# The down projection of a layer by seven block products instead of eight

## The chip, the cores and the metric

The kernel runs on one core of a Trainium2 chip. A core has five engines with an instruction queue each: TensorE (PE: matmuls from SBUF into eight banks of PSUM), VectorE (DVE), ScalarE (ACT), GpSimd (POOL) and SyncE (SP, here only transfers). The metric is device microseconds of one execution; a change is judged by several executions of both kernels on the same chip.

## What is computed

One layer on 512 tokens of width 1024, all in 32-bit floats: a token mixer of three branches, then a gated MLP with a causal convolution, each with a modulation worked out from a condition `c` and followed by a residual and a LayerNorm. The change is in the second half:

```python
D_MODEL = 1024; SEQ = 512; DEPTH = 1; D_FF = 2816; CONV_W = 3

def _conv_ffn(h, w_up, conv_w, conv_b, w_down):
    z = h @ w_up                                  # 512 x 5632
    S = z.shape[1]
    zp = jnp.pad(z, ((0, 0), (CONV_W - 1, 0), (0, 0)))
    zc = conv_b + conv_w[0] * zp[:, 0:S]
    for k in range(1, CONV_W):
        zc = zc + conv_w[k] * zp[:, k:k + S]
    val, gate = jnp.split(zc, 2, axis=-1)
    return (jax.nn.silu(gate) * val) @ w_down     # 512 x 2816 by 2816 x 1024

def reference(...):
    mod = silu(c) @ w_ada[l] + b_ada[l]
    sh_t, sc_t, gt_t, sh_f, sc_f, gt_f = jnp.split(mod, 6, axis=-1)
    ...
    h = _modulate(x, sh_f, sc_f)
    y = _conv_ffn(h, w_up[l], conv_w[l], conv_b[l], w_down[l])
    x = _layer_norm(ALPHA * x + gt_f[:, None, :] * y) * ln_f_g[l] + ln_f_b[l]
```

## The kernel before

**Products.** TensorE multiplies 32-bit numbers by a split: each operand is a rounded high part (`fp32r`, copied by ScalarE) and the rest (a difference on VectorE), and a product is three matmuls, high by low, low by high and high by high (`mm3`, L107; `mm_chunk`, L112). So every weight block costs a copy of ScalarE and a difference of VectorE before TensorE can use it. Weights come by SP's queue into a pool of three raw buffers of 128 x 1024 and are split into two buffers each of high and low parts (`wsplit`, L90; `scaled_chunk`, L1130). A planner (`make_plan`, L375) splits the chunk after the next one ahead.

**Stages in order of time.** Latent projections and attention (to about 200 us); the attention branch with the pooling inputs (`pool`, `merge(0, m)`); the pooling mixer; the spatial gating's `v` in two halves of four steps (`uv_half`, L979), where other work is hung behind the split of each step (`v_first`, `v_second`, L1004); the pooling branch (`merge(1, m)`); the spatial gating (`gated`); its branch (`merge(2, m)`); the output projection; the second modulation; the up projection of 44 chunks (22 pairs `i` of value and gate, from some 590 to 826 us); the down projection to 943 us; the normalized rows are stored while it closes.

**The up projection's end.** For each `i` ScalarE and VectorE form the convolution from PSUM, ScalarE the silu, GpSimd the product `val`; `val` (128 hidden rows x 512 tokens) is split into `f{i}h` and `f{i}l`, which stay in SBUF as the left operands.

**The down projection** is `project_out` (L1150, called at L1495) with 22 steps over the hidden dimension. Eight PSUM banks hold 4 token blocks of 128 x 2 halves of 512 columns. In 18 steps a weight row block of 128 x 1024 is loaded, multiplied by the gate `gt_f` on GpSimd (L1135, so that the gate costs nothing later), split, and used by 24 matmuls. The last four row blocks are split ahead and kept; then the banks are closed one after the other with 12 matmuls each, and `finish` (L1453) adds the residual of each bank, takes its statistics, and after both halves normalizes the row block and stores it. The last half is closed in two pieces of 256 columns.

**The gates.** `gate_rows` (L896) reduces the modulation (`ada_cols`), sends it to DRAM in one transposing transfer and reads it back as two rows spread over 128 partitions, for the mixer's gate (idx 0) and for the MLP's (idx 3).

**Pools** that the change uses: 48 tiles of 128 x 512 (`act_t`), 16 (`h_t`, the up projection's inputs until it ends), 8 (`pt_t`), 5 of 128 x 528 (`pad_t`), 8 PSUM banks (`ps`). An instruction that wants a tile waits until one is free. The order within each queue is made by the tile framework when the kernel is built; `tc.issue_after` puts an instruction behind another one of its engine, and `behind_split` puts work behind the newest weight split.

## Time and profile before

| | |
|---|---|
| median of 3 runs | 953.44 us (952.78 to 953.79) |
| the profiled execution: its own time | 953.06 us |
| its span, first to last instruction | 951.3 us |
| mean granted TensorE clock | 0.998 |
| bytes moved | 119.85 MB, 126 GB/s in the mean |
| weights of the down projection `d<-in_wdn` | 22 loads of 512 KB, 3.4 us to landing |

The profile lists each instruction with engine, line, the tile written and the tiles read, its duration, and the wait before it. "Releaser" is the instruction whose end ended a wait. Busy times of a stretch are sums over the engine's instructions in it, and a number in brackets behind them counts the instructions. PE lines are matmuls, PEld lines the loading of their left operands; a few per cent of the matmul records can be missing.

### The profile page before, as it was taken

What the parts mean: (1) busy time and instruction counts of PE and PEld (TensorE: products, weight loads), DVE (VectorE), ACT (ScalarE), POOL (GpSimd) and SP (SyncE); (2) the same over time, 40 slices, a digit from 0 to 9 for tenths busy, and PEclk for the clock granted to TensorE, in tenths of its full rate; (3) what the DMA queues carried; (4) which work ended last, traced back from release to release, by engine and by line L of the source; (5) the groups of instructions that cost most, each with busy time, mean ns of one, the idle gap of its engine ahead of it and who ended that gap; (6) DMA issues with size and microseconds to landing.
All of it is one profiled execution on the core that took longest, in us unless ns stands there. A gap on an engine that the chain in (4) does not pass through costs nothing.

```text
span 951.3 us, 12080 instructions
## 1 busy us (share of the span) xinstructions
PE 937.2 (99%) x4516; PEld 791.0 (83%) x4516; DVE 597.0 (63%) x868; ACT 377.8 (40%) x619; POOL 292.0 (31%) x270
## 2 busy tenths in 40 slices
PE   7999999999999999999999999999999999999996
PEld 6988888888888888888888889988888888888885
DVE  7966668546676575677354589575655665633277
ACT  4576555533324322133322434654444444321121
POOL 4741121122341032302043713021111132756653
PEclk9999999999999999999999999999999999999999
DMA  9823112145436532664343440233344364432322
GB/s 320 326 65 108 57 36 83 45 133 153 134 100 228 183 99 100 190 205 138 111 134 132 156 155 23 68 121 123 111 133 133 113 84 138 132 111 89 107 71 88
DMA packets 46586, 119.85 MB, mean 126 GB/s; under 512 B 6144, under 2 KB 9664, under 8 KB 46528
## 3 DMA queue, kind: packets, MB, share of 16 engines
...
q0 software_dynamic: 1024, 1.19, 0.5%
...
## 4 chain that ended last, share of the span: by engine, by line
PE 94%; DMA 2%; DVE 1%; POOL 1%; issue 1%; ACT 1%; SPq 0%; POOLq 0%; DVEq 0%; ACTq 0%
PE pzu L115 7%; PE pzu L118 7%; PE pzu L116 7%; PE py L115 4%; PE py L118 4%; PE py L116 4%; PE pg L115 4%; PE pg L116 4%; PE pg L118 4%; PE pyd L1168 3%; PE pyd L1166 3%; PE pyd L1169 3%; PE lat L528 2%; PE pu L115 2%; PE pa L115 2%; PE pa L116 2%
## 5 line engine op out<-in xcount | busy, mean ns | idle before, releaser
L95 DVE TENSOR_TENSOR wupl<-wup,wuph 128x1024 fp32r<-128x1024 f32 x38 | 47.0, 1237 | 70.9 <-PE pzu L118 40.5
L1135 POOL TENSOR_TENSOR d<-d,gtf 128x512 f32<-128x512 f32 x44 | 74.5, 1716 | 35.8 <-DMA d<-in_wdn 35.1
L1441 POOL TENSOR_TENSOR zc<-zc 128x512 f32<-128x512 f32 x22 | 29.7, 1350 | 173.6 <-ACT zc L1440 172.4
L1140 DVE TENSOR_TENSOR dl<-d,dh 128x1024 fp32r<-128x1024 f32 x18 | 29.8, 1653 | 55.8 <-PE pyd L1166 51.6
L94 ACT CAST wuph<-wup 128x1024 fp32r<-128x1024 f32 x38 | 39.8, 1048 | 46.3 <-PE pzu L116 46.3
L94 ACT CAST wbh<-wb 128x1024 fp32r<-128x1024 f32 x24 | 25.2, 1051 | 69.2 <-PE py L116 50.4
L856 DVE SCALAR_TENSOR_TENSOR ada<-adar,cact,ada 128x512 f32<-128x512 f32 x56 | 50.1, 924 | 0.0
L419 POOL TENSOR_TENSOR mg<-mg,th 128x512 f32<-128x512 f32 x16 | 29.3, 1832 | 58.6 <-DVE th L416 58.5
L95 DVE TENSOR_TENSOR wgl<-wg,wgh 128x1024 fp32r<-128x1024 f32 x22 | 28.5, 1295 | 28.5 <-ACT wgh L94 16.5
L1139 ACT CAST dh<-d 128x1024 fp32r<-128x1024 f32 x18 | 18.9, 1051 | 62.0 <-PE pyd L1169 37.8
L1421 ACT ACTIVATE zc<-pzu,cols 128x512 f32<-128x512 f32 x44 | 34.1, 778 | 22.1 <-PE pzu L118 17.7
L95 DVE TENSOR_TENSOR wbl<-wb,wbh 128x1024 fp32r<-128x1024 f32 x24 | 31.1, 1294 | 14.9 <-ACT wbh L94 6.5
L775 POOL TENSOR_SCALAR pe<-pe,mx 128x128 f32<-128x128 f32 (+3 forms) x32 | 17.0, 534 | 69.3 <-DVE mx L774 43.2
L1424 DVE SCALAR_TENSOR_TENSOR zc<-pzu,cols,zc 128x511 f32<-128x511 f32 x44 | 32.6, 744 | 4.2 <-ACT zc L1421 4.2
L94 ACT CAST wgh<-wg 128x1024 fp32r<-128x1024 f32 x22 | 23.3, 1058 | 27.9 <-PE pg L116 20.3
L1428 DVE SCALAR_TENSOR_TENSOR zc<-pzu,cols,zc 128x510 f32<-128x510 f32 x44 | 32.6, 746 | 0.8
L1440 ACT ACTIVATE zc<-zc 128x512 f32<-128x512 f32 x22 | 13.9, 631 | 43.0 <-DVE zc L1428 43.0
L926 POOL TENSOR_TENSOR asum<-apad 128x527 f32<-128x527 f32 x8 | 12.3, 1540 | 54.7 <-ACT apad L921 28.1
L298 DVE SCALAR_TENSOR_TENSOR acc<-ada,cact,acc 128x256 f32<-128x256 f32 (+1 forms) x29 | 28.3, 975 | 1.2 <-DMA ada<-in_ada1p 0.2
L416 DVE SCALAR_TENSOR_TENSOR th<-th,py 128x512 f32<-128x512 f32 x16 | 11.0, 686 | 26.3 <-PE py L118 26.3
L1113 POOL TENSOR_TENSOR oraw<-oraw,gtt 128x512 f32<-128x512 f32 x6 | 11.1, 1872 | 41.4 <-DMA oraw<-in_wo 41.4
L1135 POOL TENSOR_TENSOR o<-o,gtt 128x512 f32<-128x512 f32 x10 | 18.1, 1831 | 12.1 <-DMA o<-in_wo 10.0
...
## 6 DMA issues: line engine op xcount, KB each, us to landing
...
```

The lines of the kernel that those rows point to most:

```text
L94: nc.scalar.copy(out=hi[:, :n], in_=raw[:, :n])
L95: ins = nc.vector.tensor_tensor(out=lo[:, :n], in0=raw[:, :n], in1=f(hi[:, :n]), op=ALU.subtract)
L115: nc.tensor.matmul(o, wh[:, c], xl[k], start=k == 0, stop=False)
L116: nc.tensor.matmul(o, wh[:, c], xh[k], start=False, stop=False)
L118: nc.tensor.matmul(o, wl[:, c], xh[k], start=False, stop=k == KT - 1)
L856: nc.vector.scalar_tensor_tensor(out=acc[n], in0=src, scalar=cact[:, k : k + 1], in1=acc[n], op0=ALU.mult, op1=ALU.add,)
L1135: nc.gpsimd.tensor_tensor(out=halves[n], in0=halves[n], in1=gt[n], op=ALU.mult)
L1140: nc.vector.tensor_tensor(out=lo, in0=raw, in1=f(hi), op=ALU.subtract)
L1421: nc.scalar.activation(t, pz, AF.Identity, bias=cols[:, cc + 3 : cc + 4], scale=cols[:, cc + 2 : cc + 3])
L1424: nc.vector.scalar_tensor_tensor(out=t[:, 1:512], in0=pz[:, 0:511], scalar=cols[:, cc + 1 : cc + 2], in1=t[:, 1:512], op0=ALU.mult, op1=AL ...
L1428: nc.vector.scalar_tensor_tensor(out=t[:, 2:512], in0=pz[:, 0:510], scalar=cols[:, cc : cc + 1], in1=t[:, 2:512], op0=ALU.mult, op1=ALU.add,)
L1441: nc.gpsimd.tensor_tensor(out=val, in0=val, in1=gate, op=ALU.mult)
```

## The change

The product A·B of the down projection is cut into 2 x 2 blocks: 512 tokens into two halves, the hidden dimension into even and odd row blocks (11 pairs `p`), 1024 columns into two halves. It is then computed by seven block products instead of eight, each the sum over the pairs. The weight combinations that this needs (`t3`, `wide`, `t4`) are made from the raw weights during the earlier stages and written to DRAM; the left combinations are made when `val` is ready. The products run in two sweeps over the pairs: first products 1, 5, 6 and 7 in eight PSUM banks, then 2, 3 and 4 in six. The left operands of the second sweep go to DRAM for nine of eleven pairs and are read back. Weights of the second sweep's last five pairs are split ahead, during the first sweep. The gate now multiplies bank sums; two of the eight half rows are complete after the first sweep, the other six are completed as the second sweep's banks close. The gate rows' way through DRAM uses a transpose on VectorE and four transfers.

```diff
@@ -893,11 +894,21 @@
...
-    def gate_rows(idx, c0, name):
-        ada_cols(idx, c0, False, name)
+    def gate_line(idx, c0, name):
+        square = const.tile([P, 32], F32, name=name + "s")
+        turned = const.tile([P, 32], F32, name=name + "t")
+        nc.gpsimd.memset(square, 0.0)
+        ada_cols(idx, c0, False, name, square[:, :KT])
+        nc.vector.transpose(out=turned, in_=square)
         line = dr.tile([KT, P], F32, name=name + "r")
-        nc.gpsimd.dma_start(out=line.rearrange("j c -> c j"), in_=modulation[idx])
-        flat = line.rearrange("(o j) c -> o (j c)", o=1)
+        for i in range(4):
+            nc.gpsimd.dma_start(
+                out=line[:, 32 * i : 32 * i + 32], in_=turned[32 * i : 32 * i + KT, :]
+            )
+        gate_row[idx] = line
+
+    def gate_rows(idx, name):
+        flat = gate_row.pop(idx).rearrange("(o j) c -> o (j c)", o=1)
...
@@ -948,6 +959,32 @@
...
+    HP = NP // 2
+    wide_t = [dr.tile([P, D], F32, name=f"wt21{p}") for p in range(HP)]
+    t3_t = [dr.tile([P, 512], F32, name=f"wt3{p}") for p in range(HP)]
+    t4_t = [dr.tile([P, 512], F32, name=f"wt4{p}") for p in range(HP)]
+
+    def combine_weights(p):
+        b = []
+        for k in (2 * p, 2 * p + 1):
+            for n in range(2):
+                blk = act_t(f"wb{k}{n}", F32)
+                nc.sync.dma_start(
+                    out=blk, in_=A["wdn"][k * P : (k + 1) * P, n * 512 : (n + 1) * 512]
+                )
+                b.append(blk)
+        b11, b12, b21, b22 = b
+        for dst, x, y, op in (
+            (b22, b22, b12, ALU.subtract), (b12, b12, b11, ALU.subtract),
+            (b11, b22, b11, ALU.add), (b21, b11, b21, ALU.subtract),
+        ):
+            ins = nc.vector.tensor_tensor(out=dst, in0=x, in1=y, op=op)
+        for dst, src in (
+            (t3_t[p], b22), (wide_t[p][:, 512:], b12), (wide_t[p][:, :512], b11), (t4_t[p], b21),
+        ):
+            nc.gpsimd.dma_start(out=dst, in_=src)
+        return ins
+
...
     pool(0)
     pool(1)
@@ -957,6 +994,8 @@
             pool(m + 1)
         merge(0, m, oT_hi, oT_lo, th0[m])
         behind_split(ada_piece, 0, m)
+        if m == 6:
+            behind_split(combine_weights, 0)
...
@@ -1004,6 +1043,8 @@
     def v_second(q):
...
+        if q:
+            combine_weights(q)
...
@@ -1040,8 +1081,10 @@
...
+        if m == 4:
+            behind_split(gate_line, 0, C_GT, "gtt")
+        if m % 2:
+            behind_split(combine_weights, 4 + m // 2)
...
@@ -1089,6 +1132,8 @@
...
     for g in range(KT):
+        if g == 2:
+            gate_rows(0, "gtt")
...
@@ -1108,6 +1153,8 @@
...
+        if m < 3:
+            behind_split(combine_weights, 8 + m)
...
@@ -1402,8 +1449,61 @@
...
+    left1 = []
+    left2 = {}
+    SPILLED = HP - 2
+    spill = [[dr.tile([P, 512], F32, name=f"ys{p}{i}") for i in range(3)] for p in range(SPILLED)]
+
+    def split256(dst, src):
+        nc.scalar.copy(out=dst[:, :256], in_=src)
+        nc.vector.tensor_tensor(out=dst[:, 256:], in0=src, in1=f(dst[:, :256]), op=ALU.subtract)
+
+    def first_left(p, v1):
+        xa = act_t(f"xa{p}")
+        split256(xa, v1[:, :256])
+        left1.append([xa])
+
+    def other_lefts(p, v1, v2):
+        d = pad_t("sd")
+        e = pad_t("se")
+        for dst, x, y, op in (
+            (e[:, :256], v1[:, 256:], v2[:, 256:], ALU.add),
+            (d[:, :256], e[:, :256], v1[:, :256], ALU.subtract),
+            (d[:, 256:512], v1[:, :256], v1[:, 256:], ALU.subtract),
+            (e[:, 256:512], v2[:, :256], d[:, :256], ALU.subtract),
+        ):
...
+        split256(xs, e[:, :256])
+        nc.scalar.copy(out=xh, in_=d[:, :512])
+        nc.vector.tensor_tensor(out=xl, in0=d[:, :512], in1=f(xh), op=ALU.subtract)
+        nc.scalar.copy(out=yh, in_=v2)
+        nc.vector.tensor_tensor(out=yl, in0=v2, in1=f(yh), op=ALU.subtract)
+        split256(ys, e[:, 256:512])
+        left1[p] += [xs, xh, xl]
+        if p >= SPILLED:
+            left2[p] = [yh, yl, ys]
+            return
+        for dst, src in zip(spill[p], (yh, yl, ys)):
+            nc.gpsimd.dma_start(out=dst, in_=f(src))
...
@@ -1431,43 +1531,209 @@
...
-        if i % 2 == 1 and i < 2 * KT:
-            ada_piece(3, i // 2)
-        if i == 2 * KT:
+        if 3 <= i < 3 + KT:
+            ada_wide_piece(3, i - 3)
+        if i == 3 + KT:
             ada_parts(3, "gtf")
-        if i == 2 * KT + 2:
-            gate_rows(3, C_GT + 8, "gtf")
+        if i == 5 + KT:
+            gate_line(3, C_GT + 8, "gtf")
+        if i == 5 + KT + 1:
+            gate_rows(3, "gtf")
         nc.scalar.activation(gate, gate, AF.Silu)
         nc.gpsimd.tensor_tensor(out=val, in0=val, in1=gate, op=ALU.mult)
-        ah = act_t(f"f{i}h")
-        al = act_t(f"f{i}l")
...
-        a_hi.append(ah)
-        a_lo.append(al)
...
-
-    lnfg = row_tiles(4, act_t, "lnfg")
-    lnfb = row_tiles(5, act_t, "lnfb")
...
+        if i % 2 == 0:
+            first_left(i // 2, val)
+            held[0] = val
+        else:
+            other_lefts(i // 2, held[0], val)
+
+
+    gt_f = [gate_row[3, n] for n in range(2)]
+    R2 = 5
+    lo_half, hi_half = slice(0, 512), slice(512, 1024)
+
+    def split_wide(parts, n, name):
+        hi = wp.tile([P, D], F32R, name=name + "h", tag="whi")
+        lo = wp.tile([P, D], F32R, name=name + "l", tag="wlo")
+        for raw, c in parts:
+            nc.scalar.copy(out=hi[:, c], in_=raw)
+            nc.vector.tensor_tensor(out=lo[:, c], in0=raw, in1=f(hi[:, c]), op=ALU.subtract)
+        return hi, lo
+
...
+    def sweep_step(p, chunks):
+        for (wh, wl), users in chunks:
+            for rest in range(2):
+                for t in range(2):
+                    for acc, (xh, xl), c in users:
+                        ts_ = slice(t * P, (t + 1) * P)
+                        if rest:
+                            nc.tensor.matmul(acc[t], xh[:, ts_], wl[:, c], start=False, stop=False)
+                        else:
+                            nc.tensor.matmul(acc[t], xh[:, ts_], wh[:, c], start=p == 0, stop=False)
+                            nc.tensor.matmul(acc[t], xl[:, ts_], wh[:, c], start=False, stop=False)
+
+    m1, m5, m6, m7 = ([ps(f"pd{c}") for _ in range(2)] for c in (1, 5, 6, 7))
+
+    def lefts1(p):
+        xa, xs, xh, xl = left1[p]
+        return {
+            1: (xa[:, :256], xa[:, 256:]), 5: (xs[:, :256], xs[:, 256:]),
+            6: (xh[:, :256], xl[:, :256]), 7: (xh[:, 256:], xl[:, 256:]),
+        }
+
+    def lefts2(p):
+        yh, yl, ys = left2[p]
+        return {
+            2: (yh[:, :256], yl[:, :256]), 4: (yh[:, 256:], yl[:, 256:]),
+            3: (ys[:, :256], ys[:, 256:]),
+        }
+
+    def reload(p):
+        left2[p] = [act_t(f"z{i}{p}") for i in range(3)]
+        for dst, src in zip(left2[p], spill[p]):
+            nc.gpsimd.dma_start(out=dst, in_=src)
+
+    ws2 = {}
+
+    def second_weights(p, alloc):
+        srcs = ((2, wdn_row(2 * p + 1, lo_half)), (3, wdn_row(2 * p + 1, hi_half)), (4, t4_t[p]))
+        raws = [(c, block(src, f"dr{c}", pt_t)) for c, src in srcs]
+        ws2[p] = {c: split_block(raw, f"d{c}{p}", alloc) for c, raw in raws}
+
+    ahead = [(second_weights, HP - R2, h_t)]
+    for i in range(R2 - 1):
+        ahead += [(second_weights, HP - R2 + 1 + i, act_t), (reload, i)]
+    ahead.append((reload, R2 - 1))
+    free = 1 + 6
+    for p in range(HP - 1):
+        rb = [block(wdn_row(2 * p, lo_half), "db0"), block(t3_t[p], "db1")]
+        ra = whole(wide_t[p], "da")
+        wb_ = split_wide(zip(rb, (lo_half, hi_half)), D, "db")
+        wa_ = split_wide(((ra, slice(0, D)),), D, "da")
+        x = lefts1(p)
+        sweep_step(p, (
+            (wb_, ((m1, x[1], lo_half), (m7, x[7], hi_half))),
+            (wa_, ((m6, x[6], lo_half), (m5, x[5], hi_half))),
+        ))
+        while ahead and free >= (need := 6 if ahead[0][0] is second_weights else 3):
+            work, *args = ahead.pop(0)
+            work(*args)
+            free -= need
+        free += 4
+    p = HP - 1
+    rb = [block(wdn_row(2 * p, lo_half), "db0"), block(t3_t[p], "db1")]
...
+    for work, *args in ahead:
+        work(*args)
...
+    def ordered(work):
+        with ExitStack() as order:
+            if last_product:
+                order.enter_context(tc.issue_after(last_product[0]))
+            last_product[:] = [work().ins]
+
+    u1, u3, u4, c22 = ([None] * 2 for _ in range(4))
+
+    def evacuate(c, t, acc):
+        if c == 1:
+            u1[t] = h_t(f"u1{t}", F32)
+            nc.scalar.copy(out=u1[t], in_=acc)
+        elif c == 6:
+            u4[t] = h_t(f"u4{t}", F32)
+            nc.vector.tensor_tensor(out=u4[t], in0=acc, in1=u1[t], op=ALU.add)
+        elif c == 7:
+            u3[t] = h_t(f"u3{t}", F32)
+            nc.vector.tensor_tensor(out=u3[t], in0=acc, in1=u4[t], op=ALU.add)
+        else:
+            c22[t] = pt_t("c22")
+            nc.vector.tensor_tensor(out=c22[t], in0=acc, in1=u3[t], op=ALU.add)
+            nc.vector.tensor_tensor(out=u4[t], in0=acc, in1=u4[t], op=ALU.add)
+
+    for c, acc in ((1, m1), (6, m6), (7, m7), (5, m5)):
+        for t in range(2):
+            ts_ = slice(t * P, (t + 1) * P)
+            xh, xl = lefts1(HP - 1)[c]
+            wh, wl = ws1[c]
+            ordered(lambda: mm3(acc[t], xh[:, ts_], xl[:, ts_], wh, wl, False, True))
+            evacuate(c, t, acc[t])
+
+    def residual(t, n, q):
+        nc.vector.scalar_tensor_tensor(
+            out=x1[t][n], in0=x1[t][n], scalar=ALPHA, in1=q, op0=ALU.mult, op1=ALU.add
+        )
...
+    def whole_half(t):
+        nc.gpsimd.tensor_tensor(out=c22[t], in0=c22[t], in1=gt_f[1], op=ALU.mult)
+        residual(2 + t, 1, c22[t])
+        if t == 0:
+            statistics(2, 0, 1)
+        else:
+            for i in range(2):
+                statistics(3, i, 1, slice(i * 256, (i + 1) * 256))
+
...
+    for p in range(HP - R2):
...
+        rd = block(t4_t[p], "dd")
+        wc_ = split_wide(((rc, slice(0, D)),), D, "dc")
+        wd_ = split_wide(((rd, lo_half),), 512, "dd")
+        x = lefts2(p)
+        sweep_step(p, (
+            (wc_, ((m2, x[2], lo_half), (m3, x[3], hi_half))),
+            (wd_, ((m4, x[4], lo_half),)),
+        ))
+        if R2 + p < SPILLED:
+            reload(R2 + p)
+        if p < 2:
+            whole_half(p)
+        if p == 2:
+            lnfg = row_tiles(4, h_t, "lnfg")
+            lnfb = row_tiles(5, h_t, "lnfb")
+            q = pt_t("fq")
+            nc.gpsimd.tensor_tensor(out=q, in0=u3[1], in1=gt_f[0], op=ALU.mult)
+            residual(3, 0, q)
+
+    def final(t, n, acc, u, op, slot, eng):
+        q = pt_t("fq")
+        nc.vector.tensor_tensor(out=q, in0=u, in1=acc, op=op)
+        eng.tensor_tensor(out=q, in0=q, in1=gt_f[n], op=ALU.mult)
+        residual(t, n, q)
+        statistics(t, slot, n)
+
+    def row_end(t, count):
+        dst = x1[t]
         mv = sm.tile([P, 2], F32, name="mv", tag="mv")
-        nc.vector.bn_aggr(out=mv, in_=st[:, : D // wide].rearrange("p a b -> p (a b)"))
+        nc.vector.bn_aggr(out=mv, in_=stats[t][:, :count].rearrange("p a b -> p (a b)"))
         rs = sm.tile([P, 2], F32, name="rs", tag="rs")
         nc.vector.tensor_scalar_add(out=rs[:, 1:2], in0=mv[:, 1:2], scalar1=LN_EPS)
         nc.gpsimd.tensor_tensor(out=rs[:, 0:1], in0=rs[:, 1:2], in1=neghalf[:, 0:1], op=ALU.pow)
@@ -1492,9 +1758,46 @@
...
 
-    project_out(
-        lambda k: A["wdn"][k * P : (k + 1) * P, :], NP, 4, a_hi, a_lo, [gate_row[3, n] for n in range(2)], h_t, finish, "d", narrow=True
-    )
+    def close(c, acc, t, cols_=slice(0, 512), start=False):
+        ts_ = slice(t * P, (t + 1) * P)
+
+        def products():
+            for p in range(HP - R2, HP):
+                xh, xl = lefts2(p)[c]
+                wh, wl = ws2[p][c]
+                ins = mm3(
+                    acc, xh[:, ts_], xl[:, ts_], wh[:, cols_], wl[:, cols_],
+                    start and p == HP - R2, p == HP - 1,
+                )
+            return ins
+
+        ordered(products)
...
+    last_product.clear()
+    for t in range(2):
+        eng = (nc.gpsimd, nc.vector)[t]
+        close(2, m2[t], t)
+        final(t, 0, m2[t], u1[t], ALU.add, 0, nc.gpsimd)
+        close(3, m3[t], t)
+        final(t, 1, m3[t], u4[t], ALU.add, 1, eng)
+        row_end(t, 2)
+        if t == 0:
+            close(4, m4[0], 0)
+            final(2, 0, m4[0], u3[0], ALU.subtract, 1, nc.gpsimd)
+            row_end(2, 2)
+    halves = (slice(0, 256), slice(256, 512))
+    close(4, m4[1][:, :256], 1, halves[0])
+    extra = ps("pe4x")
+    close(4, extra[:, :256], 1, halves[1], True)
+    q = pt_t("fq")
+    nc.vector.tensor_tensor(out=q, in0=m4[1], in1=gt_f[0], op=ALU.mult)
+    nc.vector.tensor_tensor(out=x1[3][0], in0=x1[3][0], in1=q, op=ALU.subtract)
+    statistics(3, 2, 0, halves[0])
+    q = pt_t("fq")
+    nc.vector.tensor_tensor(out=q[:, :256], in0=extra[:, :256], in1=gt_f[0][:, 256:], op=ALU.mult)
+    nc.vector.tensor_tensor(out=x1[3][0][:, 256:], in0=x1[3][0][:, 256:], in1=q[:, :256], op=ALU.subtract)
+    statistics(3, 3, 0, halves[1])
+    row_end(3, 4)
```

More of the change, by code (lines that the diff above doesn't have):

```diff
@@ L882, in trunk, with ada_cols @@
     ada_quarters = {}
-    def ada_cols(idx, c0, one, name):
-        dst = const.tile([P, KT], F32, name=name + "c")
+    def ada_cols(idx, c0, one, name, dst=None):
+        if dst is None:
+            dst = const.tile([P, KT], F32, name=name + "c")
         nc.vector.tensor_reduce(
@@ new lines, in whole, with block, split_block @@
+    def whole(src, name):
+        raw = wp.tile([P, D], F32, name=name, tag="raw", bufs=3)
+        nc.sync.dma_start(out=raw, in_=src)
+        return raw
+    def block(src, name, alloc=pad_t):
+        raw = alloc(name)
+        nc.sync.dma_start(out=raw[:, :512], in_=src)
+        return raw[:, :512]
+    def split_block(raw, name, alloc):
+        hi = alloc(name + "h")
+        lo = alloc(name + "l")
+        nc.scalar.copy(out=hi, in_=raw)
+        nc.vector.tensor_tensor(out=lo, in0=raw, in1=f(hi), op=ALU.subtract)
+        return hi, lo
@@ new lines, in trunk @@
+    p = HP - 1
+    rb = [block(wdn_row(2 * p, lo_half), "db0"), block(t3_t[p], "db1")]
+    ra = whole(wide_t[p], "da")
+    ws1 = {
+        c: split_block(raw, f"d{c}", h_t)
+        for c, raw in ((1, rb[0]), (7, rb[1]), (6, ra[:, :512]), (5, ra[:, 512:]))
+    }
+    for work, *args in ahead:
+        work(*args)
+    stats = [sm.tile([P, 4, 6], F32, name=f"std{t}", tag=f"std{t}", bufs=1) for t in range(TT)]
+    last_product = []
+    def ordered(work):
[3 more added lines that the diff above has]
+            last_product[:] = [work().ins]
```

46 lines of the change are left out of this document (24 added, 22 removed).

## The prediction

> **What bounds the kernel now.** I read the shares of the span first, then the chain that ended last, then busy time by stretches.
>
> ```profile
> span 951.3 us, 12080 instructions
> ...
> PE 937.2 (99%) x4516; PEld 791.0 (83%) x4516; DVE 597.0 (63%) x868; ACT 377.8 (40%) x619; POOL 292.0 (31%) x270
> ...
> PE 94%; DMA 2%; DVE 1%; POOL 1%; issue 1%; ACT 1%; SPq 0%; POOLq 0%; DVEq 0%; ACTq 0%
> ```
> ```profile
> core 0: us, PE busy (x) PEld busy (x) DVE busy (x) ACT busy (x) POOL busy (x), PEclk, DMA share, GB/s
> 320.00:340.00 20.00, 20.00 (x90) 16.55 (x89) 12.86 (x17) 5.10 (x7) 0.00 (x0) 1.00 0.50 150
> 340.00:360.00 20.00, 20.00 (x90) 16.59 (x89) 15.04 (x19) 4.22 (x4) 8.79 (x6) 1.00 0.29 94
> 680.00:700.00 20.00, 20.00 (x90) 16.53 (x90) 11.13 (x15) 9.51 (x12) 2.59 (x2) 1.00 0.37 124
> 840.00:860.00 20.00, 20.00 (x90) 16.55 (x89) 6.17 (x4) 3.15 (x3) 13.80 (x9) 1.00 0.30 97
> ```
>
> TensorE is busy in 99% of the span and makes 94% of the chain. In these four stretches it has no gap at all, and its clock is 1.00. So a matmul taken out shortens the kernel by its spacing, as long as nothing else comes late; and work put on the other engines is free until it makes TensorE wait. The last stretch is the down projection: there VectorE is busy for 6.17 of 20 us, ScalarE for 3.15, and the transfers take 0.30 of the DMA engines.
>
> The end of the kernel is the other place to read, instruction by instruction:
>
> ```profile
> 921.45 0.39 PE L108 MATMUL pyd<-d18l,f18h 128*128 128x512 f32 x1
> ...
> 940.49 0.28 PE L108 MATMUL pyd<-d18l,f18h 128*128 128x256 f32 x1
> ...
> 943.24 0.28 PE L110 MATMUL pye<-d21h,f21h 128*128 128x256 f32 x1
> 943.69 0.43 DVE L1468 BATCH_NORM_STATS2 std<-out 128x6 f32<-128x256 f32 x1
> 944.03 0.40 DVE L1467 TENSOR_TENSOR out<-out,pye 128x256 f32<-128x256 f32 x1
> 944.47 0.43 DVE L1468 BATCH_NORM_STATS2 std<-out 128x6 f32<-128x256 f32 x1
> ```
>
> 84 matmuls of 512 columns start between 921.45 and 940.49, so their spacing is 19.04 / 84 = 0.2267 us (the 0.39 is one matmul's passage through the array). The 24 narrow ones run from 940.49 to about 943.36, 0.1196 apart. TensorE ends at 943.24 + 0.28 = 943.52; VectorE has the last statistics at 944.90, 1.38 later; from there to 951.3 it is 6.4 us of normalizing and storing, which the change leaves as it is.
>
> **Matmuls removed.** The old form has 4 token blocks x 2 halves x 22 rows x 3 = 528 products of 512 columns, of which 12 are done as 24 narrow ones: 516 x 0.2267 + 24 x 0.1196 = 119.9 us. The new form has 7 block products x 2 token blocks x 11 pairs x 3 = 462, 15 of them as 30 narrow ones: 447 x 0.2267 + 30 x 0.1196 = 104.9 us. **Saved: 14.9 us.** The stages are then: first sweep 11 x 24 x 0.2267 = 59.9, streamed second sweep 6 x 18 x 0.2267 = 24.5, closings 75 x 0.2267 + 30 x 0.1196 = 20.6.
>
> **The end, added.** In the closings VectorE now forms each bank's sum, and the gate multiplies banks rather than weights. The prices:
>
> ```profile
> L416 DVE SCALAR_TENSOR_TENSOR th<-th,py 128x512 f32<-128x512 f32 x16 | 11.0, 686 | 26.3 <-PE py L118 26.3
> ...
> L1258 DVE SCALAR_TENSOR_TENSOR x<-x,rs,lntb 128x512 f32<-128x512 f32 x8 | 5.6, 745 | 0.4 <-POOL rs L135 0.4
> ...
> L1468 DVE BATCH_NORM_STATS2 std<-out 128x6 f32<-128x512 f32 x6 | 4.2, 692 | 0.1
> ...
> L1470 DVE BATCH_NORM_AGGREGATE mv<-std 128x2 f32<-128x12 f32 x3 | 0.6, 209 | 0.1
> ...
> L1472 DVE TENSOR_SCALAR rs<-mv 128x1 f32<-128x1 f32 x4 | 0.6, 154 | 0.1
> ```
> ```profile
> 934.29 1.41 DVE L1475 SCALAR_TENSOR_TENSOR out<-out,mv,lnfg 128x512 f32<-128x512 f32 x2
> ```
> ```profile
> 805.56 1.29 POOL L1441 TENSOR_TENSOR zc<-zc 128x512 f32<-128x512 f32 x1 [9.65 <-ACT zc L1440]
> ```
>
> Count from the end of the first closing (call it 0). The last matmul is 4 x 15 x 0.2267 + 30 x 0.1196 = 17.2 later. VectorE's work after 0: four halves whose gate is on GpSimd (bank sum 0.69, residual from SBUF 0.75, statistics 0.69: 2.13 each, 8.5); one whose gate it does itself (0.69 more: 2.82); the last half in two pieces (0.69 + 0.69 + 0.43, then 0.40 + 0.40 + 0.43: 3.04); three row ends (0.21 + 0.15 + 1.41 + 0.75 = 2.52, 7.56). Sum 21.9. In the first two halves it has nothing else to do while GpSimd multiplies: 1.29 and some 0.2 of hand-over, twice, 3.0. So its last statistics are 21.9 + 3.0 - 17.2 = 7.7 after the last matmul, against 1.38 now: **6.3 us added**. Before, a half cost it only 0.69 + 0.69, and eight closings of 12 x 0.2267 = 2.7 gave it time for that. Low end: no waits, and starts a twentieth closer than the durations, as in the row of L1475, where two take 1.41 and not 2 x 0.745: 20.8 - 17.2 - 1.38 = 2.2; a gain is excluded, since the work is longer than the time for it. High end: the four gate multiplies and three last additions of GpSimd each hold up VectorE, by the difference of the next two rows, 1.1 each: 6.3 + 7.7 = 14.
>
> ```profile
> L1445 DVE TENSOR_TENSOR f19l<-zc,f19h 128x512 fp32r<-128x512 f32 x1 | 1.8, 1778 | 0.0
> ...
> L1445 DVE TENSOR_TENSOR f2l<-zc,f2h 128x512 fp32r<-128x512 f32 x1 | 0.7, 694 | 0.4 <-ACT f2h L1444 0.4
> ```
>
> f19l was slow while GpSimd multiplied weights. I stay at 6.3, since most of GpSimd's work falls into VectorE's waits. The Trainium skill (SBUF — State Buffer, section "SBUF: two separate sides") calls the port pair that the two share an exclusive lock, so that the later one blocks for the whole of the other's instruction; the two rows agree, and by it the end term is the 14 (rival 5).
>
> **The weights' supply.** Gating leaves the weights' path, so GpSimd's 44 multiplies go; TensorE did not wait for them, so that alone brings nothing. Transfers grow. A first-sweep pair loads 1.05 MB; five times 0.79 MB of second weights and five reloads of 0.79 MB come on top: 19.4 MB. The second sweep loads 6 x 0.79 and reloads 4 x 0.79: 7.9 MB. Together 27.3 MB in 84.4 us, 323 GB/s, against:
>
> ```profile
> 30.00:40.00 10.00, 10.00 (x60) 9.08 (x60) 9.72 (x10) 6.05 (x15) 7.53 (x7) 1.00 1.05 381
> 296.00:301.00 5.00, 5.00 (x24) 4.14 (x23) 3.18 (x6) 1.05 (x1) 0.00 (x0) 1.00 0.76 249
> 301.00:306.00 5.00, 5.00 (x24) 4.15 (x23) 4.49 (x7) 1.05 (x1) 0.77 (x1) 1.00 1.01 375
> ```
>
> A full DMA moves 375 to 381 GB/s, so the sweeps need some 86% of it; first weights come in ahead, during the up projection (0.37 busy). I take 0.5 us, with bounds of 0 and, at 312 (midway between 249 and 375), 3.1. Splitting costs VectorE 2 x 0.69 + 1.24 + 3 x 0.69 = 4.7 of a pair's 5.4 us where it also splits ahead (f2l above for 512 columns, the first row below for 1024).
>
> ```profile
> L95 DVE TENSOR_TENSOR wupl<-wup,wuph 128x1024 fp32r<-128x1024 f32 x38 | 47.0, 1237 | 70.9 <-PE pzu L118 40.5 <-ACT wuph L94 24.8 <-ACT f18h L1444 2.8
> ...
> L1314 DVE TENSOR_TENSOR h2T7l<-h2f,h2T7h 128x256 fp32r<-128x256 f32 x2 | 0.9, 426 | 0.8 <-ACT h2f L1307 0.8
> ```
>
> **The change of sweeps.** All eight banks are full in the first sweep and six are wanted in the second. ScalarE copies two out, VectorE adds the other six into three tiles with 2 + 2 + 4 instructions: 8 x 0.69 = 5.5 us beside the last pair's 24 x 0.2267 = 5.4 us of matmuls. The wait added is TensorE's for a free bank; behind it stands the whole second sweep. Behind VectorE's eight stand the first second-sweep splits, which TensorE waits for too. But the banks come free in the order in which they are closed, and the second sweep wants its last two only 12 matmuls in, 2.7 us. I take 0.5, bounds 0 and 5.5.
>
> **Beside the earlier stages.** Eleven weight combinations add 4 x 0.69 = 2.8 us of VectorE each, and 1.05 MB in and 1.05 MB out. In 320 to 340 VectorE has 12.86 of 20 busy; three of them add 8.3 over three steps of 24 x 0.2267 = 5.4, which it just holds. Transfers there rise from 1.05 to 3.15 MB a step, 579 GB/s, so the DMA falls behind by 3.3 MB, 8.9 us; three raw weight buffers, a step each, cover that (16 us). Without that cover it would be up to 8.9 us of waiting. The left operands cost VectorE 7 x 0.42 + 2 x 0.69 = 4.3 a pair instead of 1.4, over 21.8 us of matmuls: from 56% (680 to 700) to some 70%. GpSimd issues 44 stores of combinations, 27 of left operands and 27 reloads:
>
> ```profile
> L903 POOL DMA_DIRECT2D gtf<-gtfr x2 | 1.2, 582 | 2.0 <-DMA gtfr<-gtfc 2.0
> ```
>
> 98 x 0.58 = 57 us, spread over 700 us in which GpSimd is mostly idle and loses the 44 weight multiplies; behind them in its queue stand the additions of the branches and the up projection's products, which are wanted a chunk of 5.4 us or a sweep later. The gate's row for the mixer goes out in four small transfers instead of one and is asked for some 50 us ahead of its first use; the wide pieces of the last modulation are the same instructions on other tiles; both at nothing. I take 0.5 for all of this; bounds 0 and 3.
>
> **Sum.** -14.9 + 6.3 + 0.5 + 0.5 + 0.5 = -7.1. The profiled execution took 953.06 (span 951.3 and 1.8 around it), 0.04% below the median of 953.44, so I sum against it: **946.0 us**.
>
> **The rivals.**
> 1. *The end is not late* (VectorE keeps pace; the low end of 2.2, and 0.5 for the other terms): 953.06 - 14.9 + 2.7 = 940.9. For it: now VectorE is only 1.38 behind. Against it: 21.9 us of work in 17.2.
> 2. *The DMA cannot feed the sweeps*: the one that ends slower. Place: the two sweeps; price: 27.3 MB at 249 GB/s (the row of 296 to 301) are 110 us, 25 more than the matmuls, giving 971. It decides from 27.3 / (84.4 + 7.1) = 298 GB/s down. For it: the loads alternate with reloads of what was written before, small blocks, two queues. Against it: 375 beside a busy TensorE.
> 3. *The side work is not hidden*: SP's queue, in order, has the combinations' loads ahead of weight loads, and VectorE waits for them. With the 8.9 us above: 954.9, no change. For it: 579 GB/s asked. Against it: three buffers.
> 4. *The change of sweeps stands*: the 5.5 us of emptying shows in full: 951.0. For it: VectorE has the splits too. Against it: the order in which banks come free. The quoted stretches have no pause, and a clock of 1.00. The Trainium skill (TensorE: Matmul & The Clock Gate, "Part 1: The HAM clock gate (the "warmup" mystery)") says that after some 3.4 us of idling the array runs at half clock until it has been busy as long again; by an estimate from that page the 951.0 would be 952.7.
> 5. *GpSimd holds VectorE up in the end*: the 14 in full: 953.06 - 14.9 + 14 + 1.5 = 953.7, no change. For it: f19l. Against it: GpSimd mostly multiplies while VectorE waits for just that. This is where the rule of the SBUF page leads if every meeting costs its full time.
>
> That the products are not fewer is no rival: they are counted in the code.
>
> **How the numbers follow.** Forecast (942.5 to 950): 0.58. Rival 1: 0.13. Rival 2: 0.09. Rival 3: 0.07. Rival 4: 0.08. Rival 5: 0.05. For the range I add the bounds: the lowest is 953.06 - 14.9 + 2.2 = 940.4, and a little under it for the reading of the spacing; at the top the end's 14 alone gives 952.2, and the small terms' upper bounds with 6.3 give 956, which need not meet. 940.0 to 952.5 leaves out rivals 2 and 5 and most of rival 3, some 0.2. A measurement of this kernel tells about 0.2% (1.9 us) from no change. Faster by more: the forecast, rival 1 and most of rival 4, 0.78; within: rival 5 and most of rival 3, 0.11; slower: rival 2 and the rest of 3 and 4, 0.11.
>
> **What would show it.** Right: 462 equivalents of down products at 0.2267 without gaps; the last statistics 6 to 9 us after the last matmul, VectorE without idle time in the last 15 us; DMA share 0.8 to 0.95 through the sweeps. Wrong: gaps of TensorE before a first- or second-sweep matmul that end on a cast or difference which itself waited for a transfer (rival 2); gaps between 320 and 390 (rival 3); one gap where the second sweep begins (rival 4); VectorE's residuals and centrings at 1.8 instead of 0.7 in the end (rival 5); a last statistic within 3 us of the last matmul (rival 1). The forecast would be wrong above all if VectorE's order in the closings lets row ends wait behind GpSimd twice.

## The result, and the profile after

The changed kernel takes 957.9 us (median of four executions, 957.09 to 958.89) against 953.1 of the kernel before, measured beside it: 1.005 times the time, with a 95% interval of 1.0037 to 1.0062. It is slower by 0.5%. The forecast was 946.0 us, with a range of 940.0 to 952.5.

The profiled execution took 957.47 us. Its page (span, busy time by engine, chain of work by engine):

```profile
span 955.7 us, 12643 instructions
...
PE 926.9 (97%) x4453; PEld 780.4 (82%) x4453; DVE 676.0 (71%) x1043; ACT 408.6 (43%) x689; POOL 279.2 (29%) x339
...
PE 82%; DVE 7%; DMA 6%; POOL 2%; issue 1%; ACT 1%; SPq 0%; DVEq 0%; POOLq 0%; ACTq 0%
```

TensorE is busy for 10.3 us less than before, and yet the span is 4.4 us longer. The list of what TensorE waited for has a new first row (the three numbers: us in total, times, the longest); the stretches of 10 us show where (columns as in the prediction: each engine's busy time, then the granted clock, the share of the DMA engines and GB/s):

```profile
PE pd L1592 <- ACT dbh L1559: 6.9, 1, 6.9
```
```profile
820.00:830.00 10.00, 4.50 (x20) 3.38 (x18) 3.87 (x7) 2.33 (x4) 1.26 (x1) 0.83 0.02 7
830.00:840.00 10.00, 8.56 (x26) 6.32 (x27) 6.94 (x13) 6.77 (x11) 0.00 (x0) 0.66 0.82 270
840.00:850.00 10.00, 10.00 (x46) 8.29 (x45) 6.77 (x10) 6.42 (x10) 1.66 (x3) 1.00 0.95 305
```

One wait of 6.9 us, before the first matmul of the down projection, on ScalarE's rounding of the first weights (dbh). Behind it the clock is low: only 26 matmuls are recorded in 830 to 840, against 46 in the next stretch. Why the rounding is late is in the order of ScalarE's queue (its timeline around the gap; in brackets the idle time before an instruction and what ended it):

```profile
824.53 0.78 ACT L1521 ACTIVATE zc<-pzu,cols 128x512 f32<-128x512 f32 x1 [4.66 <-PE pzu L118]
826.97 0.63 ACT L1542 ACTIVATE zc<-zc 128x512 f32<-128x512 f32 x1 [1.66 <-DVE zc L1528]
829.04 0.62 ACT L1481 CAST yh<-zc 128x512 fp32r<-128x512 f32 x1 [1.44 <-POOL zc L1543]
829.56 0.40 ACT L1458 CAST xs<-se 128x256 fp32r<-128x256 f32 x1
830.17 0.62 ACT L1479 CAST xh<-sd 128x512 fp32r<-128x512 f32 x1 [0.20 <-DVE sd L1475]
830.69 0.61 ACT L1559 CAST dbh<-db 128x512 fp32r<-128x512 f32 x1
```

ScalarE idled for 4.66 us up to 824.53. But the rounding of the first down weights stands, in program order, behind the last up-projection pair's whole chain: activation, VectorE's convolution, SiLU, GpSimd's product, and then three roundings of that pair's left operands, which nobody needs before the end of the first sweep. The weights themselves were long there: their two loads were issued at 815.33 and 815.81, and loads into these tiles took 3.4 to 5.5 us to land. In the kernel before, ScalarE rounds the first two row blocks of down weights, at 816.71 and 821.91, ahead of the last chunk's activation (823.73), and so before the up projection ends:

```profile
816.71 1.04 ACT L1139 CAST dh<-d 128x1024 fp32r<-128x1024 f32 x1
...
821.91 1.06 ACT L1139 CAST dh<-d 128x1024 fp32r<-128x1024 f32 x1 [2.36 <-PE pzu L116]
823.73 0.78 ACT L1421 ACTIVATE zc<-pzu,cols 128x512 f32<-128x512 f32 x1 [0.76 <-PE pzu L118]
```

In the changed kernel TensorE ran out of up-projection work at 824.11 + 0.23 = 824.34 and started again at 831.36. Its first down matmul, the first streamed one of the second sweep and the last of all:

```profile
831.36 0.80 PE L1592 MATMUL pd<-dbh,xa 128*128 128x512 f32 x1 [6.86 <-ACT dbh L1559]
...
894.15 0.39 PE L1592 MATMUL pe<-dch,z 128*128 128x512 f32 x1
...
939.84 0.28 PE L110 MATMUL pe4x<-d410h,yh 128*128 128x256 f32 x1
```

Piece by piece the span reads so. A matmul is counted as ended 0.23 us after its start, a narrow one 0.12 after; the gap at 824 counts as part of the down projection:

| | before | changed | e9 (below) |
|---|---|---|---|
| up projection ends | 823.53 | 824.34 | 823.25 |
| down projection, from there to the end of its last matmul | 119.8 | 115.6 | 105.0 |
| of it, up to the first streamed matmul of the second sweep | - | 69.8 | 59.9 |
| from there to the end of the span | 7.9 | 15.7 | 15.8 |

The first sweep's 264 matmuls want 264 x 0.2267 = 59.9 us and took 69.8: 9.9 us lost at the start. The end grew by 7.8 us, where 6.3 were forecast. Of the rest, 0.7 us went in the second sweep and 0.8 before the down projection. The 0.8 can't be put down to the change: in e3, e4 and e8 below, whose code is the same up to there, the up projection ends at 823.51, 823.47 and 822.85.

### The profile page after: what moved, and what is told of

Same layout as the page of the kernel before. It is cut to its first block, busy times and chain, and to the rows that moved or that the text cites. A ratio compares the mean times of both kernels' runs of the same rounds, so it can differ in the third digit from the quotient of the medians.

```text
span 955.7 us, 12643 instructions
## 1 busy us (share of the span) xinstructions
PE 926.9 (97%) x4453; PEld 780.4 (82%) x4453; DVE 676.0 (71%) x1043; ACT 408.6 (43%) x689; POOL 279.2 (29%) x339
## 4 chain that ended last, share of the span: by engine, by line
PE 82%; DVE 7%; DMA 6%; POOL 2%; issue 1%; ACT 1%; SPq 0%; DVEq 0%; POOLq 0%; ACTq 0%
PE pzu L116 7%; PE pzu L118 7%; PE pzu L115 7%; PE pg L115 4%; PE pg L116 4%; PE pg L118 4%; PE py L118 4%; PE py L115 4%; PE py L116 4%; PE pd L1590 2%; PE pd L1592 2%; PE pd L1593 2%; DMA ada<-in_ada1p 2%; PE pa L115 2%; PE pu L115 2%; PE pu L116 2%
## 5 line engine op out<-in xcount | busy, mean ns | idle before, releaser
L95 DVE TENSOR_TENSOR wupl<-wup,wuph 128x1024 fp32r<-128x1024 f32 x38 | 52.4, 1379 | 24.2 <-PE pzu L118 15.9
L985 POOL DMA_DIRECT2D wt<-wb x44 | 24.5, 556 | 77.1 <-DVE wb L981 72.0
L981 DVE TENSOR_TENSOR wb<-wb,wb 128x512 f32<-128x512 f32 x44 | 35.3, 806 | 6.2 <-DMA wb<-in_wdn 5.7
L856 DVE SCALAR_TENSOR_TENSOR ada<-adar,cact,ada 128x512 f32<-128x512 f32 x42 | 38.7, 961 | 0.4 <-DMA adar<-in_ada 0.4
L1614 POOL DMA_DIRECT2D z<-ys x27 | 14.6, 542 | 56.7 <-PE pd L1590 35.0
L771 ACT ACTIVATE pe<-sc,mx 128x128 f32<-128x128 f32 (+3 forms) x32 | 16.8, 528 | 8.8 <-DVE mx L769 7.5
```

The lines of the kernel that those rows point to most:

```text
L95: ins = nc.vector.tensor_tensor(out=lo[:, :n], in0=raw[:, :n], in1=f(hi[:, :n]), op=ALU.subtract)
L856: nc.vector.scalar_tensor_tensor(out=acc[n], in0=src, scalar=cact[:, k : k + 1], in1=acc[n], op0=ALU.mult, op1=ALU.add,)
L981: ins = nc.vector.tensor_tensor(out=dst, in0=x, in1=y, op=op)
```

## The experiments

All are compared with the kernel before, on the same chip; behind each time stand its ratio to the kernel before and the 95% interval. An edit "on e5" stands on that kernel, any other on the changed kernel. Of the edits only the lines that matter are shown.

**e1, the first split ahead.**

```diff
...
                 mm_chunk(pz, uh, ul, h2_hi, h2_lo)
+            if m == 2 * NP - 1:
+                rb, ra = first_loads(0)
+                wb0 = split_b(rb)
             cc = C_CONV + 4 * m
...
         val, gate = half
+        if i == NP - 1:
+            wa0 = split_a(ra)
...
```

> Edit: the first pair's weight loads and splits stand ahead of the last up product's activation, everything else as after the change. Theory A (order of ScalarE's and VectorE's queues at the start of the down projection costs 6.9 us of gap and some 3 us of half clock): the gap before the first down matmul falls under 1 us, its spacing is 0.23 from the start, and the time is 957.9 - 10 = 948 us (947 to 950), so faster than before by 0.5%. Theory B (SyncE's queue: the loads of the second weights that stand in front of the second pair's first weights, 816.8 to 829.0, are the cause): the first gap goes but one of some 5 us opens before the second pair, 953 or more. Theory C (no free buffer): the gap stays, 957.9.

Measured: 952.3 us, 0.9996 of before (0.9984 to 1.0008). About 5 us came back, not 10. The gap at 824 is gone; two others opened. TensorE's and then ScalarE's timeline (of an execution of 954.8 us, above the median of 952.3, so its gaps may be longer than usual):

```profile
830.71 0.50 PE L1608 MATMUL pd<-dbh,xa 128*128 128x512 f32 x1 [1.83 <-ACT dbh L1512]
846.24 0.50 PE L1608 MATMUL pd<-dbh,xa 128*128 128x512 f32 x1 [3.95 <-ACT dbh L1512]
```
```profile
829.52 0.62 ACT L1479 CAST xh<-sd 128x512 fp32r<-128x512 f32 x1 [0.20 <-DVE sd L1475]
830.04 0.61 ACT L1512 CAST dbh<-db 128x512 fp32r<-128x512 f32 x1
...
841.71 0.62 ACT L1595 CAST d27h<-dr 128x512 fp32r<-128x512 f32 x1 [4.92 <-DMA dr<-in_wdn]
843.73 0.62 ACT L1595 CAST d37h<-dr 128x512 fp32r<-128x512 f32 x1 [1.40 <-DMA dr<-in_wdn]
845.05 0.62 ACT L1595 CAST d47h<-dr 128x512 fp32r<-128x512 f32 x1 [0.70 <-DMA dr<-wt]
845.57 1.13 ACT L1512 CAST dbh<-db 128x512 fp32r<-128x512 f32 x2
```

The same fault one pair on, twice: the second pair's weights stand behind the last left operands (xh), and the fourth pair's behind second-sweep weights (d27h to d47h), which are wanted some 70 us later and whose loads landed late. Theory C (no free buffer) falls, and theory A was right in kind but counted one place where there are several. B's gap before the second pair is there, but of 1.83 us and not some 5; the longer one stands two pairs on. On SyncE's queue the wide loads of the second to fourth pair stood ahead of the second pair's blocks, and one of them waited for a buffer:

```profile
SPq L1518 <- DVE dal L1513: 12.1, 3, 10.5
```

**e2, the second weights later** (the prefetch loop begins with `while p and ahead`, so one pair later).

> Edit: the first set of second-sweep weights is asked for one pair later; the first split stays behind the last left operands. Theory A: SyncE is no longer held from 816.8 to 829.0, but the gap of 6.9 us before the first down matmul stays, 957.9 us (956.5 to 958.5). Theory B: the gap goes, 948 us.

Measured: 957.0 us, 1.004 (1.0027 to 1.0052), with the gap of 6.9 us as it was. But the edit didn't free SyncE: the loads came out in nearly the same order, and it still waited for GpSimd's last product:

```profile
SPq L1570 <- POOL zc L1543: 12.2, 1, 12.2
```

So this run agrees with A and says nothing against B.

**e3, the gap filled.**

```diff
         x = lefts1(p)
+        if p == 0:
+            for _ in range(30):
+                nc.tensor.matmul(m1[0], x[1][0][:, :P], h2_hi[0], start=True, stop=True)
```

> Edit: 30 matmuls of 128 x 512 whose result is overwritten stand ahead of the first down matmul and fill the gap; nothing else. Theory of the clock (the 0.43 us spacing from 833.7 to 836.7 comes from TensorE's idle 6.9 us): the first down matmul starts at about 831.4 as after, is spaced 0.23 from the start, and the end comes 3 us earlier, 955 us. Rival (the late splits pace those matmuls, not the clock): spacing stays 0.43 where weights are late, 957.9 us or up to 1 us more.

Measured: 955.3 us, 1.0021 (1.0011 to 1.0031), 0.3% under the changed kernel, as its theory had forecast. The two timelines of TensorE, the changed kernel first:

```profile
834.58 0.63 PE L1593 MATMUL pd<-dbh,xa 128*128 128x512 f32 x1
835.00 0.63 PE L1592 MATMUL pd<-dbh,xh 128*128 128x512 f32 x1
...
836.71 0.45 PE L1593 MATMUL pd<-dah,xl 128*128 128x512 f32 x1
837.00 0.39 PE L1592 MATMUL pd<-dah,xs 128*128 128x512 f32 x1
```
```profile
823.51 6.96 PE L1636 MATMUL pd<-h2T0h,xa 128*128 128x512 f32 x30
830.58 0.50 PE L1592 MATMUL pd<-dbh,xa 128*128 128x512 f32 x1
...
833.16 0.39 PE L1593 MATMUL pd<-dbh,xa 128*128 128x512 f32 x1
833.38 0.40 PE L1592 MATMUL pd<-dbh,xh 128*128 128x512 f32 x1
...
834.30 0.39 PE L1593 MATMUL pd<-dah,xl 128*128 128x512 f32 x1
```

After an idle gap the spacing is 0.42 (834.58 to 835.00); with the gap filled it is 0.22 (833.16 to 833.38), while the edit adds nothing but the filling matmuls. So the half speed comes from the idling. From the end of the up projection to the second wide-weight matmul (dah,xl) it is 836.71 - 824.34 = 12.37 in the one and 834.30 - 823.51 = 10.79 in the other: 1.6 us of clock. The Trainium skill (TensorE: Matmul & The Clock Gate, "Part 1: The HAM clock gate (the "warmup" mystery)") says this of an idle array, and that it lasts about 3.4 us; the half clock here ended at 837.00, 5.6 us after the start, in which waits lie too. Over the whole first sweep e3 gained less than that, 69.4 against 69.8 us, in part because the faster matmuls then waited for a later rounding (0.8 us). The two profiled spans differ by 1.2 us, of which 0.8 lie before the gap, where the two kernels are equal. So only 0.4 of the 2.8 us that the times differ by is seen to come from the edit, and the forecast time was met in part by chance.

**e4, gates ahead.** The copied sums u1, u3, u4 are gated and added to the residual in the streamed second sweep, since gate x (u + M) is gate x u + gate x M (u the kept sum of the first sweep, M the bank that closes last); a closed bank is then gated by VectorE alone.

```diff
...
-    def final(t, n, acc, u, op, slot, eng):
+    def final(t, n, acc, op, slot):
         q = pt_t("fq")
-        nc.vector.tensor_tensor(out=q, in0=u, in1=acc, op=op)
-        eng.tensor_tensor(out=q, in0=q, in1=gt_f[n], op=ALU.mult)
-        residual(t, n, q)
+        nc.vector.tensor_tensor(out=q, in0=acc, in1=gt_f[n], op=ALU.mult)
+        nc.vector.tensor_tensor(out=x1[t][n], in0=x1[t][n], in1=q, op=op)
         statistics(t, slot, n)
...
```

> Edit: in the closings nothing is summed before the gate: the copied sums of the first sweep are gated and added to the residual in the streamed second sweep, and a closed bank is gated by VectorE and added. Theory D (GpSimd's gate and VectorE's waits for it, 1.5 us twice, and its slower instructions beside GpSimd make the end late): from the last matmul to the end 15.6 becomes 11 to 13 us, 953.5 to 956 us. Rival E (VectorE's own amount of work, 21 us against 17.2 us of closings, makes it late): 14.5 us or more, 957 us. Rival F (the moved work makes gaps in the second sweep): TensorE's gaps there grow from 0.9 to 2 us or more and eat the gain.

Measured: 955.3 us, 1.0016 (1.0006 to 1.0025). Theory D and rival F are both right: the end fell from 15.7 to 11.1 us, and of the 4.6 a part went back into the second sweep, which became 2.9 us longer, with gaps of 1.1, 0.7 and 0.4 us, where VectorE is now full:

```profile
900.00:910.00 10.00, 8.05 (x33) 5.69 (x32) 10.00 (x13) 3.25 (x4) 8.45 (x10) 1.00 1.10 352
```

Another 0.9 us went in the first sweep, at 879.59, on a rounding of wide weights; it is there in e8 too (0.8), and why isn't shown.

**e5, the loads in order**, on e1.

```diff
...
-        rb = [block(wdn_row(2 * p, lo_half), "db0"), block(t3_t[p], "db1")]
-        return rb, whole(wide_t[p], "da")
+        rb = [pad_t("db0")[:, :512], pad_t("db1")[:, :512]]
+        nc.sync.dma_start(out=rb[0], in_=wdn_row(2 * p, lo_half))
+        second = nc.sync.dma_start(out=rb[1], in_=t3_t[p])
+        with tc.issue_after(second.ins):
+            ra = whole(wide_t[p], "da")
+        return rb, ra
...
```

> Edit: as e1, and on SyncE's queue each pair's wide load stands behind the same pair's two block loads (in e1 the wide loads of the second and third pair stood ahead of the second pair's blocks and held the queue for 10.5 us waiting for a buffer). Theory A2 (two orders cost the start: the splits behind the last left operands, and the loads behind a wide load that waits for a buffer): e1's two gaps of 5.8 us shrink to under 1.5, 952.3 - 5 = 947.5 us (946 to 949), faster than before by 0.6%. Rival B2 (the DMA cannot deliver what the first pairs and the prefetch together ask for in their 5.4 us each): gaps of 4 us or more stay in 840 to 850 and the time stays at 951 to 952.

Measured: 951.4 us, 0.9978 (0.9968 to 0.9987). The wait of 3.95 fell to 0.7; the one of 1.83 stayed, and here it brought half the clock with it (0.83 in 830 to 840). A2's 947.5 was missed. B2's time, 951 to 952, was met, but not its mechanism: the DMA then delivered 396 GB/s in 840 to 850, and no gap of 4 us stood there. What is left at the second pair isn't the loads: its two block loads were issued at 812.41 and 818.80, and the rounding ran only at 830.03, right behind the last left operand's.

**e6, the prefetch later** (on e5: none before the third pair, then one set or reload a pair, later two).

> Edit: as e5, and the second-sweep weights are asked for from the third pair on, one set or reload a pair. Theory A2: no more than 1 us better than e5, 947 us (945.5 to 948.5). Rival B2: only this one closes the gap in 840 to 850, 947 against 951 of e5.

Measured: 951.4 us, 0.9978 (0.9968 to 0.9987), as e5. So behind e5 the place of the prefetch isn't what still costs; no profile of this run is read.

**e7, both**, and **e8, gates ahead, late.** The gates of e4 are asked for after the last streamed pair of the second sweep, in e7 on e6, in e8 on the changed kernel.

> Edit: as e6, and the copied sums are gated and added to the residual right after the streamed part of the second sweep, where VectorE is busy for under 4 of 10 us, instead of in 890 to 910 as in e4; closed banks are gated by VectorE. If start and end are independent and e4's gaps in the second sweep came from where the work stood: e6 less 4.5 us, 942.5 us (941 to 944.5), faster than before by 1.1%. If the moved work collides again: e6 less 1 us or less, 946 us.

> Edit: the end of e7 alone, on the changed kernel with its gap at the start. The tail from the last matmul to the end is 11 us as in e4 (15.6 in the changed kernel), and e4's gaps of some 3 us in the second sweep are gone: 957.9 - 4.5 = 953.4 us (952.5 to 955). Rival: VectorE, with 5 x 0.75 us more to do before the first closing's sum, is late again, tail 13 us or more, 955.5 us.

Measured: e7 950.0 us, 0.9959 (0.9945 to 0.9974); e8 955.3 us, 1.0018 (1.0008 to 1.0028), no better than e4. Both forecasts were missed. The tail is 11.2 us in both, but the gaps in the second sweep stayed. GpSimd's and VectorE's timelines of e8:

```profile
908.34 3.84 POOL L1728 TENSOR_TENSOR fq<-u,gtf 128x512 f32<-128x512 f32 x2 [1.35 <-DVE x L1688]
```
```profile
908.71 2.30 DVE L1560 TENSOR_TENSOR dcl<-dc,dch 128x1024 fp32r<-128x1024 f32 x1
910.94 1.79 DVE L1560 TENSOR_TENSOR ddl<-dd,ddh 128x512 fp32r<-128x512 f32 x1
...
913.25 1.22 DVE L1560 TENSOR_TENSOR dcl<-dc,dch 128x1024 fp32r<-128x1024 f32 x1
914.39 0.68 DVE L1560 TENSOR_TENSOR ddl<-dd,ddh 128x512 fp32r<-128x512 f32 x1
```

The gates, ready since the change of sweeps, were put into the queues ahead of the place where the code asks for them, among the splits. While GpSimd multiplies (908.34 to 912.18) the same two splits take 2.30 and 1.79 instead of 1.22 and 0.68: 1.1 more each, the difference that the prediction had read from f19l. The Trainium skill (SBUF — State Buffer, "SBUF: two separate sides") calls this an exclusive lock; the rows agree. This pair of splits ends in a gap of 0.4 us at 912.78. The longer gaps of e8, 1.1 at 902.88 and 0.65 at 907.04, end on splits that stood behind residuals of 1.77 and 1.78 us, the same loss beside GpSimd.

**e9, the second pair too**, on e5. The first pair's matmuls and the split of the second pair's blocks are written behind the last product on GpSimd and ahead of the last left operands:

```diff
...
+        if i == NP - 1:
+            m1, m5, m6, m7 = ([ps(f"pd{c}") for _ in range(2)] for c in (1, 5, 6, 7))
+            first_step(0, wb0, wa0)
+            rb, ra = first_loads(1)
+            wb1 = split_b(rb)
         if i % 2 == 0:
             first_left(i // 2, val)
...
```

> Edit: as e5, and the first pair's matmuls and the split of the second pair's blocks stand ahead of the last pair's SiLU and left operands too (in e5 that split stood behind them: a gap of 1.8 us at 830.7 and half the clock up to 840). Theory A3 (what is left of the start's loss is the same queue order, one pair on, and its clock): no gap over 0.3 us in 820 to 840, PEclk 1.00, and 951.4 - 1.8 - 0.7 - 1.5 = 947.5 us (946.5 to 949). Rival B3 (the DMA): the gap moves on by one or two pairs, 950.5 to 951.5.

Measured: 945.8 us, 0.9919 (0.9903 to 0.9935). Theory A3 holds, with a time 0.7 us under its range, and nothing moved on:

```profile
820.00:830.00 10.00, 10.00 (x46) 8.28 (x45) 6.33 (x11) 4.81 (x8) 1.59 (x1) 1.00 0.27 93
830.00:840.00 10.00, 10.00 (x45) 8.27 (x45) 8.64 (x15) 7.30 (x12) 1.66 (x3) 1.00 0.93 312
840.00:850.00 10.00, 10.00 (x46) 8.26 (x45) 6.39 (x9) 5.24 (x9) 1.61 (x3) 1.00 1.08 399
...
880.00:890.00 10.00, 10.00 (x46) 8.29 (x45) 8.50 (x11) 2.01 (x3) 7.96 (x11) 1.00 1.13 393
```

TensorE has no gap and a clock of 1.00 through both sweeps, and the first sweep takes 59.9 us, as counted. The DMA engines are full (0.93 to 1.13 in 830 to 900), yet TensorE never waits for them; ScalarE does, for up to 3.0 us, on second-sweep weights that aren't wanted yet. The first streamed matmul of the second sweep and the last of all:

```profile
883.15 0.39 PE L1552 MATMUL pe<-dch,z 128*128 128x512 f32 x1
...
928.10 0.28 PE L110 MATMUL pe4x<-d410h,yh 128*128 128x256 f32 x1
```

**e10, the gates by VectorE**, on e9. The five gates that e4 moved go to VectorE, behind the last streamed split:

```diff
...
+    ins = last_lo[0]
+    for row, n, u in ((0, 0, u1[0]), (0, 1, u4[0]), (2, 0, u3[0]), (1, 0, u1[1]), (1, 1, u4[1])):
+        with tc.issue_after(ins):
+            nc.vector.tensor_tensor(out=u, in0=u, in1=gt_f[n], op=ALU.mult)
+        ins = residual(row, n, u).ins
...
```

> Edit: as e9, and the copied sums are gated by VectorE, behind the last split of the streamed second sweep, instead of by GpSimd in the middle of it (e7: gaps of 2.3 us in 890 to 910 with GpSimd busy for 9.8 and VectorE for 9.1 to 10.0). Theory D2 (e7's gaps come from the splits being held up beside GpSimd, and VectorE is idle enough in 910 to 925 for 5 x 1.44 = 7.2 us): no gap beyond the changed kernel's 0.15 in 890 to 910, tail 11 to 11.5 us, e9 - 4.3 = 943.2 us (942 to 944.5). Rival E2 (the 7.2 us make VectorE late in the closings): tail 13 us, 945.5.

Measured: 941.2 us, 0.987 (0.9853 to 0.9888), the fastest of all, 1.3% under the kernel before, and 4.6 us under e9, all of it at the end (15.8 to 11.2). D2 holds: no gap of TensorE in 890 to 910, and VectorE takes the work where it idled (in e9 it was busy for 2.93 us of 900 to 910):

```profile
890.00:900.00 10.00, 10.00 (x45) 8.26 (x45) 7.54 (x12) 4.70 (x6) 2.03 (x4) 1.00 0.96 317
900.00:910.00 10.00, 10.00 (x46) 8.27 (x45) 7.64 (x11) 1.57 (x2) 0.00 (x0) 1.00 0.00 1
```

**e11, the row ends offloaded**, on e10 (in row blocks 0 and 2 both halves are scaled by ScalarE and added to by GpSimd).

> Edit: as e10, and in the ends of row blocks 0 and 2 ScalarE scales and GpSimd adds for both halves, not for one. VectorE has 2 x 0.74 us less: if its backlog alone makes the tail, 1.3 us less than e10, 942 us. If GpSimd's four additions hold VectorE up for more than that (its pairs of centrings took 2.4 and 2.1 us beside GpSimd in the changed kernel against 1.4 alone): equal to e10 or up to 1 us more.

Measured: 941.3 us, 0.9873 (0.9857 to 0.9888), as e10. What VectorE saves (2 x 0.74), it loses beside GpSimd: in that end a bank's addition of 0.69 takes 1.78, and another, at 920.02, takes 1.80, against 0.69 in e10.

```profile
924.94 1.78 DVE L1762 TENSOR_TENSOR x<-x,fq 128x512 f32<-128x512 f32 x1
```

**e12, without the load order**: e9 with e1's loads.

> Edit: as e9 without the order between wide loads and block loads: the first pair's matmuls and two pairs' block splits stand ahead of the last left operands, SyncE's queue as it comes out of that. If the splits' place is what counted (theory A3): as e9, 946 us (945 to 947.5), no gap over 0.3 us. If the loads' order counted as much: the wide load of the fourth pair, waiting for a buffer ahead of the third pair's blocks, leaves a gap of 2 to 4 us near 834 or 845, 948.5 to 951 us.

Measured: 947.8 us, 0.9938 (0.9922 to 0.9955). That lies between the two forecasts. It has one gap, of 0.6 us at 855.53, not the 2 to 4 that the loads' order would have made; there the rounding of wide weights stood behind a second-sweep weight's, which had waited 1.7 us for its load. The medians of e9 and e12 differ by 2.0 us, but the intervals overlap, so what the loads' order is worth beyond the splits' place isn't settled.

## Why the prediction was wrong, point by point

*The start of the down projection* is the step that failed. The prediction gave it no term and no rival; it only said that "first weights come in ahead, during the up projection", and its signs of being wrong had a gap on a cast only where the cast waits for a transfer. The loads did come ahead: they were issued at 815. The splitting did not, because it is queued on ScalarE and VectorE behind the last pair's left operands, which the change adds: 8 instructions on VectorE and 4 on ScalarE that were counted as load (4.3 us a pair) but not as a place in a queue. The kernel before had its first two roundings ahead of the up projection's last work; the change lost that place. It cost 9.9 us: 7.0 of gap and 2.9 of half clock (1.6 by e3) and late splits behind it. e1 moves the first pair's splits and its gap goes; e9 moves the second pair's too, with the loads in order, and the time is 945.8 (947.8 in e12, without that order).

*Matmuls removed, 14.9 us*: right. In e9 the down projection takes 105.0 us against 119.8 before, 14.8 less.

*The end, 6.3 us added*: right in kind, 7.8 measured. VectorE's last statistics came 945.78 - 940.12 = 5.7 us after TensorE's end, less than the 7.7 forecast. What was missing lies behind them: the 6.4 us of normalizing and storing were taken to stay, but became 9.9, since row blocks 1 and 3 are both finished there, one after the other. The sum had the third row end (2.52) ahead of the last statistics; it ran behind them (VectorE's timeline of the changed kernel):

```profile
946.00 1.41 DVE L1741 SCALAR_TENSOR_TENSOR x<-x,mv,lnfg 128x512 f32<-128x512 f32 x2
...
947.39 1.41 DVE L1741 SCALAR_TENSOR_TENSOR x<-x,mv,lnfg 128x512 f32<-128x512 f32 x2
948.71 3.28 DVE L1753 SCALAR_TENSOR_TENSOR x<-x,rs,lnfb 128x512 f32<-128x512 f32 x3
```

The closing doubt of the prediction, row ends behind GpSimd, was that in part: e4, e8 and e10, without GpSimd's gates, end 11.1 to 11.2 us after the last matmul.

*Supply, change of sweeps and side work, 0.5 each*: together about nothing, by e9. Beside the matmuls (-14.8) and the end (+7.9), e9's span leaves 944.0 - 951.3 + 14.8 - 7.9 = -0.4. Rival 2 (the DMA) falls: in e9 the sweeps ran at 312 to 399 GB/s in 830 to 900 with no wait of TensorE on a transfer. Rivals 3 and 4 fall too, as no gap stands at 320 to 390 or at the change of sweeps. Rival 1 falls with the 15.7 us at the end. Rival 5 was there in part: two pairs of centrings took 2.42 and 2.07 us in the end instead of 1.41, and without GpSimd's gates, and so without VectorE's waits for them, the end is 4.6 us shorter (e4). But the end as a whole grew by 7.8 and not by its 14.

That e9 comes out at the forecast 946.0 is partly chance: an end 1.5 us dearer and three small terms of 1.5 us that were nothing cancel.
